# A hybrid decoder layer on one core: the convolution's last tap and bias from GpSimd to ScalarE

## The chip, the cores and the metric

The kernel runs on 1 core of one Trainium2 chip. A core has five engines that work side by side and wait for each other through semaphores: TensorE (PE in the profile; its weight loads are PEld), VectorE (DVE), ScalarE (ACT), GpSimd (POOL) and SyncE (SP), which here only issues DMAs. TensorE multiplies out of SBUF into banks of PSUM; VectorE and ScalarE read PSUM and SBUF. In this kernel GpSimd reads and writes SBUF alone. The metric is device time in microseconds from launch to end, as the median of several runs. A profile is of one execution more; it has a span, from its first to its last instruction, and a time of its own.

## The reference, cut to what matters

One layer (DEPTH is 1) of a trunk with two groups of heads, on a prompt of 2048 tokens and on 8 samples of one token, with D_MODEL 1024:

```python
ada = silu(c) @ w_ada + b_ada
shift, scale, gate = split(ada, 3)
hn = rmsnorm(x, g_norm) * (1 + scale) + shift
xa, za, q, k, v, glr, zg = split(hn @ w_in, SPLITS)

xp = concatenate([conv0, xa], axis=1)                    # 3 rows of the past, then xa
xc = conv_b + sum(xp[:, j:j + T] * conv_w[j] for j in range(4))
gx = sigmoid(xc @ w_gate_x + b_gate_x)                   # by blocks of 128 columns
ga = sigmoid(xc @ w_gate_a + b_gate_a)
log_a = 8 * ga * log_sigmoid(lru_lambda)
u = sqrt(-expm1(2 * log_a)) * (gx * xc)
h = scan(h = exp(log_a) * h + u)
y_lru = h * silu(za)

y_gla = rmsnorm(gated_linear_attention(q, k, v, glr)) * silu(zg)
x = x + gate * (concatenate([y_lru, y_gla]) @ w_out)
y = rmsnorm(x, g_final)
```

All data is float32. The change touches the line of `xc` (conv_w has four taps, the last of which multiplies the token's own `xa`), and, elsewhere, the sum `+ b_ada` for `gate`.

## The kernel before, in words

Activations lie with their features on the 128 partitions and tokens along the free axis. A float32 product is made of three fp32r products: each operand is split into a rounded high part (ScalarE) and the rest (VectorE), and hi*hi, hi*lo, lo*hi are added in PSUM. `project` (L636 to L649) does that for one tile of 128 columns of w_in and one segment of tokens: 24 matmuls into one of four PSUM banks called `acc`, at L642 to L644.

The prompt is worked in two halves of 1024 tokens. The first half has two segments of 512; the second has three, of 384, 384 and 264 (256 tokens of the prompt and the 8 samples). In each half the four GLA heads take turns with groups of RG-LRU tiles (`LRU_TILES`). The last two tiles of the second half come on their own, at L1606 to L1616, while the first operands of the output projection are already being prepared. From about 1122 us on the output projection (L1476) runs alone.

For one RG-LRU tile, `xa_unit` (L1232) projects a segment, lets ScalarE copy the bank to `xa` (L1244; three columns of the past stand ahead of it), and calls `conv` (L1130). There GpSimd writes `cv` = first tap times `xa` + bias (L1136), and VectorE adds the other three taps in place (L1138). With the past's three columns ahead, tap k reads `xa` from column c0 + k on; the last tap, k = 3, reads just the columns that the copy wrote. ScalarE then rounds `cv` to `xh` (L1161, or L1154 where it comes later) and VectorE makes the rest, `xl` (L1162, L1155). The eight samples of the second half have their own small steps (L1147, L1149). `gates` (L1164) comes two or three units later: six matmuls per segment into two banks (L1174 to L1176), ScalarE's Tanh out of them (L1177), then Exp, Tanh and Sqrt (L1181 to L1184, each change of function table costs a load), and on VectorE the products L1188 to L1190 and the scan L1192. L1188 is the last reader of `cv`. `xa`, `xh`, `xl` and `cv` have one buffer each, so a tile's `cv` is written when the tile before has been through L1188.

In the middle of the two halves `modulate` (L180) prepares the second half's input: PE transposes (L188), ScalarE applies scale and shift by partition out of PSUM (L190, L191, the function Identity), GpSimd rounds (L192), VectorE takes the rest (L193). At the start L209 is the same kind of step.

`out_weights` (L718) multiplies the gate into w_out and builds the sums that the last stage needs, in the gaps of all this. It works in two column halves. `begin(q)` loads the gate (`g`, L725), its bias (`bt`, L726) and the first weights, and four units later `add` (L729) adds the bias (L730). `bt` shares the one buffer of tag "t" with the sums of the step before.

What sets the order: the source calls things in an order of units. `after(u, f)` queues f until u units have passed, `tick` advances the count and calls what is due. Beneath that, the framework plans the order of each engine's queue from its own estimates of when each instruction would be ready; the order of the source is a priority. Inside an engine's queue the chip keeps the planned order: an instruction that waits holds up those behind it. Two things pin the plan: `in_order` ties every instruction of a block to the one before on its engine, and `behind(q)` (L662) ties what is issued under it behind the newest instruction that the source has put on engine q. SyncE's queue of DMAs is planned the same way. PSUM banks are given out by the plan, too: an `acc` tile takes whichever of the four banks comes free.

Of the kernel before, what the change touches and what calls it, by code (L numbers as in the profile page):

```python
# [11 lines left out]
AF = mybir.ActivationFunctionType  # L12
OP = mybir.AluOpType
# [31 lines left out]
def dram(ap, off, pattern):  # L45
    return bass.AP(tensor=ap.tensor, offset=ap.offset + off, ap=pattern)
# [3 lines left out]
def hybrid_kernel(ctx, tc, i, o):  # L50
    nc = tc.nc
    V, S, G, PE, SP = nc.vector, nc.scalar, nc.gpsimd, nc.tensor, nc.sync
# [365 lines left out]
    with tc.tile_pool(name="ada", bufs=1, side="right") as ap:  # L418
# [79 lines left out]
        with in_order():  # L498
# [24 lines left out]
            for c in range(1, 4):  # L523
                k = (2 * c, 2 * c + 1)
# [111 lines left out]
    def project(w, c0, n, mid=None):  # L636

        hi, lo, _ = w
        ps = acc()
        for kt in range(KT):  # L640
            a, b = hh[:, kt, c0:c0 + n], hl[:, kt, c0:c0 + n]
            PE.matmul(ps[:, :n], hi[:, kt], a, start=kt == 0, stop=False)  # L642
            PE.matmul(ps[:, :n], hi[:, kt], b, start=False, stop=False)  # L643
            PE.matmul(ps[:, :n], lo[:, kt], a, start=False, stop=kt == KT - 1)  # L644
            if mid and kt == 3:
                mid()
            if kt % 2:
                drip()
        return ps[:, :n]  # L649
# [12 lines left out]
    def behind(q):  # L662

        return tc.issue_after(next(x for x in reversed(list(nc.cur_bb.bb.instructions)) if x.engine == q.engine))
# [5 lines left out]
    def after(units, fn, gla=False):  # L670
        clock[1] += 1
        heapq.heappush(pend, (clock[0] + units, clock[1], fn, gla))

    def tick(units=1.0):
        clock[0] += units
        while pend and pend[0][0] <= clock[0]:
            heapq.heappop(pend)[2]()
# [40 lines left out]
    def out_weights():  # L718


        def begin(q):

            g = hp.tile([P, 2, 256], F32, tag="g", name="g")
            bt = hp.tile([P, 2, 256], F32, tag="t", name="bt")
            SP.dma_start(g, dram(gated, (8 + 32 * q) * 256, [[0, P], [64 * 256, 2], [1, 256]]))  # L725
            SP.dma_start(bt, dram(i["b_ada"], 2 * D + q * 256, [[0, P], [512, 2], [1, 256]]))  # L726
            r = load(8 * q)

            def add():  # L729
                V.tensor_tensor(g, g, bt, op=OP.add)  # L730
                after(0.5, lambda: step(8 * q, r, g))

            after(4, add)

        def where(s):

            return s // 8, s // 4 % 2, s % 4

        def load(s):
            q, f, m = where(s)  # L740
            r = hp.tile([P, 2, 2, 256], F32, tag="r", name="r")
            for a in range(2):
                k = CTS[f] + 4 * a + m
                SP.dma_start(r[:, a], i["w_out"][0, k * P:(k + 1) * P].rearrange("p (b n) -> p b n", b=2)[:, :, q * 256:q * 256 + 256])
            return r

        def one(ops, end):


            if phase[0] == 1:  # L750
                after(0.5, lambda: one(ops, end))
                return
            with behind(V):
                for f in ops[0]:
                    f()
            after(0.5, (lambda: one(ops[1:], end)) if ops[1:] else end)

        def step(s, r, g):
            t = hp.tile([P, 3, 256], F32, tag="t", name="t")
            b11, b12, b21, b22 = r[:, 0, 0], r[:, 0, 1], r[:, 1, 0], r[:, 1, 1]  # L760
            q, f, m = where(s)
            c = slice(q * 256, q * 256 + 256)

            def op(*a):
                return lambda: V.tensor_tensor(*a[:3], op=a[3])

            def split(n, x):
                p = hp.tile([P, 2, 256], F32R, tag="p", name="p", bufs=2)
                S.copy(p[:, 0], x)
                V.tensor_tensor(p[:, 1], x, p[:, 0].bitcast(F32), op=OP.subtract)  # L770

                def store2():
                    for h in range(2):
                        SP.dma_start(wd2[n, :, h, m, c], p[:, h].bitcast(F32))

                after(1.5, store2)

            def store():

                for x, ops in ((r[:, 0], (B11, T1)), (r[:, 1], (B21, B22)), (t, (T2, T3, T4))):  # L780
                    for n, k in enumerate(ops):
                        if not (f and k in (B22, T4)):
                            SP.dma_start(wd[f, k, :, m, c], x[:, n])
                if s % 8 < 7:
                    after(1, lambda: again(s + 1, g))
                elif q == 0:
                    after(1, lambda: begin(1))

            one([[op(r[:, 0], r[:, 0], g, OP.mult)], [op(r[:, 1], r[:, 1], g, OP.mult)],
                 [op(t[:, 1], b22, b12, OP.subtract), op(b12, b12, b11, OP.subtract)],  # L790
                 [op(t[:, 0], b22, b12, OP.subtract), op(t[:, 2], b21, t[:, 0], OP.subtract)]]
                + ([[lambda: split(0, b22)], [lambda: split(1, t[:, 2])]] if f else []), lambda: after(1, store))

        def again(s, g):
            r = load(s)
            after(1.5, lambda: step(s, r, g))

        begin(0)
# [322 lines left out]
    def lru_units(half, last_a=None):  # L1121
# [5 lines left out]
        def t_(tag, dt=F32, extra=0):  # L1127
            return lp.tile([P, TH + NS + extra], dt, tag=tag, name=tag)

        def conv(j, s, xa, cv, xh, xl):  # L1130
            c0, sn = SEGS[half][s]
            c = slice(c0, c0 + sn)
            cq = slice(c0, min(c0 + sn, TH))
            cw = [vecT[:, j, R_CW + k:R_CW + k + 1] for k in range(4)]
            cb = vecT[:, j, R_CB:R_CB + 1]
            G.tensor_scalar(cv[:, cq], xa[:, cq], cw[0], cb, op0=OP.mult, op1=OP.add)  # L1136
            for k in range(1, 4):
                V.scalar_tensor_tensor(cv[:, cq], xa[:, cq.start + k:cq.stop + k], cw[k], cv[:, cq],  # L1138
                                       op0=OP.mult, op1=OP.add)
            if c.stop >= TH:  # L1140
                if half == 0:
                    V.tensor_copy(xac[:, j], xa[:, TH:TH + 3])
                else:
                    V.tensor_copy(stT[:, j, 0:3], xa[:, TH:TH + 3])
                    V.tensor_copy(stT[:, j, 4:12], xa[:, TH + 3:TH + 3 + NS])
                    cs = vecT[:, j, R_CONV:R_CONV + 24].rearrange("p (b k) -> p b k", k=3)
                    V.tensor_scalar(cv[:, sm], xa[:, TH + 3:TH + 3 + NS], cw[3], cb, op0=OP.mult, op1=OP.add)  # L1147
                    for k in range(3):
                        V.scalar_tensor_tensor(cv[:, sm], cs[:, :, k], cw[k], cv[:, sm],  # L1149
                                               op0=OP.mult, op1=OP.add)  # L1150

            def split():
                with behind(S):
                    S.copy(xh[:, c], cv[:, c])  # L1154
                V.tensor_tensor(xl[:, c], cv[:, c], xh[:, c].bitcast(F32), op=OP.subtract)  # L1155

            if last_a or half == 0 and j == LRU_TILES[3][-1]:

                after(2, split)
            else:  # L1160
                S.copy(xh[:, c], cv[:, c])  # L1161
                V.tensor_tensor(xl[:, c], cv[:, c], xh[:, c].bitcast(F32), op=OP.subtract)  # L1162
# [69 lines left out]
        def xa_unit(t, s):  # L1232
            j = t.j
            if s == 0:
                t.xh = t_("xh", F32R, 48)
                t.one = lp.tile([P, 1], F32, tag="one", name="one")
                t.xl, t.xa, t.cv = t_("xl", F32R), t_("xa", extra=8), t_("cv")
                if half == 0:
                    V.memset(t.xa[:, :3], 0.0)
                else:  # L1240
                    V.tensor_copy(t.xa[:, :3], xac[:, j])
            c0, sn = SEGS[half][s]
            ps = project(t.wx, c0, sn)
            S.copy(t.xa[:, 3 + c0:3 + c0 + sn], ps)  # L1244
            conv(j, s, t.xa, t.cv, t.xh, t.xl)
            tick()
            if last_a is None:
                after(3 if j == LRU_TILES[3][-1] or half == 1 else 2, lambda: gates(t, [s]))
            elif s == len(SEGS[half]) - 1:
                after(3 if j == LRU_TILES[3][-1] else 2, lambda: gates(t, range(s + 1)))  # L1250
# [4 lines left out]
        def za_unit(t, s):  # L1255
# [3 lines left out]
            tick()  # L1259

        return xa_load, xa_unit, za_load, za_unit

    def lru(half, js):
# [539 lines left out]
    for n in range(2, 16):  # L1803
        g = n - 1
# [17 lines left out]
    for q in range(8):  # L1822
        g, k = 2 + q // 2, q % 2
# [63 lines left out]
```

## Time and profile before

| | us |
|---|---|
| median of 3 runs | 1462.96 |
| the three runs | 1461.14, 1462.96, 1467.99 |
| profiled execution: its time | 1460.23 |
| profiled execution: its span | 1458.5 |
| busy in the span: PE / DVE / ACT / POOL | 1431.1 / 1002.3 / 632.3 / 95.9 |
| mean granted TensorE clock | 0.997 |

The profile's page gives busy time of each engine, the chain of waits that ended last, and groups of instructions by line of the source. A group's row reads: line, engine, operation, output and inputs by the program's names with shape, count; then busy time, the mean of one in ns; then the idle time of the engine just before those instructions and what ended it. A row of the waits reads: who waited for whom, us in total, how often, the longest. A row of the timeline reads: start, duration, engine, line, operation, and in square brackets the engine's idle time before it and its releaser. Matmuls overlap in their pipeline, so the durations of single matmuls add up to more than their share of the time; idle time of PE is what counts.

### The profile page before, as it was taken

The numbers are of one execution on the slowest core, as the hardware profiler recorded it, in microseconds if no ns is written. First come the engines' busy times: TensorE is split into PE (matmuls) and PEld (weight loads), VectorE is DVE, ScalarE is ACT, GpSimd is POOL, SyncE is SP. The second block draws the span as 40 slices with busy tenths as digits, with TensorE's granted clock in tenths as the row PEclk, the third lists the DMA queues.
The fourth block names the chain that finished last, engine by engine and source line by source line (L and its number), as shares of the span: only waits on it lengthen the run. The fifth ranks groups of instructions, "written<-read, shape, count | busy, mean of one in ns | idle before, by whom it ended". The sixth has DMA issues, their size and how long they took to land.

```text
span 1458.5 us, 23166 instructions
## 1 busy us (share of the span) xinstructions
PE 1431.1 (98%) x8753; PEld 1269.5 (87%) x8753; DVE 1002.3 (69%) x2390; ACT 632.3 (43%) x1137; POOL 95.9 (7%) x116
## 2 busy tenths in 40 slices
PE   7999999999999999999999999999999999999997
PEld 6888888888898888999999999999998887788886
DVE  5756555765766778667567656576678986688886
ACT  4642532652454376533532552345156522154332
POOL 1200000100100013001001101010011000000000
PEclk9999999999999999999999999999999999999999
DMA  9755544645555664245644535463552767694452
GB/s 332 261 177 173 191 163 145 211 138 183 169 193 185 204 207 152 95 137 164 213 139 168 179 134 177 163 200 128 188 200 82 281 227 274 227 349 143 139 172 102
DMA packets 173606, 268.53 MB, mean 184 GB/s; under 512 B 10483, under 2 KB 126867, under 8 KB 171054
## 3 DMA queue, kind: packets, MB, share of 16 engines
q1 hardware_dynamic: 141093, 250.00, 50.3%
q10 hardware_dynamic: 32048, 16.00, 3.7%
q8 instruction: 69, 1.13, 0.3%
q0 software_dynamic: 352, 1.05, 0.2%
q14 instruction: 44, 0.35, 0.1%
HBM read 168.55 MB, written 98.52 MB: 183 GB/s over the span
## 4 chain that ended last, share of the span: by engine, by line
PE 48%; DVE 4%; ACT 2%; DMA 1%; POOL 0%; issue 0%; SPq 0%; ACTq 0%; DVEq 0%
PE acc L1476 12%; PE tp L1476 9%; PE acc L642 6%; PE acc L644 6%; PE acc L643 6%; PE acc L327 2%; PE acc L328 2%; PE acc L329 1%; DVE cv L1138 1%; PE po L975 1%; PE pss L1682 1%; PE tp L1040 0%; DMA w<-parts 0%; POOL cv L1136 0%; PE tp L941 0%
## 5 line engine op out<-in xcount | busy, mean ns | idle before, releaser
L642 PE MATMUL acc<-hh,w 128*128 128x384 f32 (+2 forms) x1256 | 446.7, 356 | 2.2 <-DMA w<-parts 1.3
L643 PE MATMUL acc<-hl,w 128*128 128x384 f32 (+2 forms) x1256 | 435.4, 347 | 0.0
L644 PE MATMUL acc<-hh,w 128*128 128x384 f32 (+2 forms) x1256 | 434.6, 346 | 0.0
L642 PEld LDWEIGHTS acc<-hh,w 128*128 128x128 f32 x1256 | 236.2, 188 | 24.2 <-DVE xb L881 3.0
L644 PEld LDWEIGHTS acc<-hh,w 128*128 128x128 f32 x1256 | 236.2, 188 | 19.4
L643 PEld LDWEIGHTS acc<-hl,w 128*128 128x128 f32 x1256 | 236.3, 188 | 19.2 <-issue 0.4
L1476 PE MATMUL acc<-w,a 128*128 128x512 f32 (+1 forms) x792 | 184.8, 387 | 0.0
L1476 PEld LDWEIGHTS acc<-w,a 128*128 128x128 f32 x792 | 146.9, 188 | 33.1 <-issue 3.4
L327 PE MATMUL acc<-w,hh 128*128 128x256 f32 (+1 forms) x508 | 145.8, 287 | 0.1
L329 PE MATMUL acc<-w,hl 128*128 128x256 f32 (+1 forms) x508 | 143.6, 283 | 0.2 <-DVE hl L216 0.2
L328 PE MATMUL acc<-w,hh 128*128 128x256 f32 (+1 forms) x508 | 143.4, 282 | 0.0
L1476 PE MATMUL tp<-w,a 128*128 128x512 f32 x564 | 136.1, 391 | 0.0
L1476 PEld LDWEIGHTS tp<-w,a 128*128 128x128 f32 x564 | 105.4, 188 | 26.7 <-issue 5.1
L1030 ACT ACTIVATE zs<-acc 128x512 f32<-128x512 f32 (+2 forms) x80 | 41.1, 513 | 173.9 <-PE acc L644 173.6
L1031 DVE SCALAR_TENSOR_TENSOR zs<-zs,acc 128x512 f32<-128x512 f32 (+2 forms) x80 | 46.3, 579 | 79.6 <-ACT zs L1030 79.4
L327 PEld LDWEIGHTS acc<-w,hh 128*128 128x128 f32 x508 | 96.3, 189 | 1.7 <-DVE vl L859 0.4
L329 PEld LDWEIGHTS acc<-w,hl 128*128 128x128 f32 x508 | 96.2, 189 | 0.4 <-DVE hl L216 0.4
L1138 DVE SCALAR_TENSOR_TENSOR cv<-xa,vecT,cv 128x512 f32<-128x512 f32 (+2 forms) x120 | 77.1, 650 | 27.4 <-POOL cv L1136 27.1
L328 PEld LDWEIGHTS acc<-w,hh 128*128 128x128 f32 x508 | 95.6, 188 | 0.2
L1136 POOL TENSOR_SCALAR cv<-xa,vecT 128x512 f32<-128x512 f32 (+2 forms) x40 | 49.0, 1224 | 607.2 <-ACT xa L1244 483.8
L1326 ACT CAST a<-s 128x512 fp32r<-128x512 f32 x61 | 36.5, 620 | 95.6 <-issue 36.2
L858 ACT CAST vh<-acc 128x256 fp32r<-128x256 f32 x56 | 20.7, 370 | 90.1 <-PE acc L329 71.1
(341 smaller groups left out, 2246.0 us busy)
## 6 DMA issues: line engine op xcount, KB each, us to landing
w<-parts SPq DMA_DIRECT2D x38, 1024.0 KB
parts<-w SPq DMA_DIRECT2D x37, 1024.0 KB
wr<-in_w_in_dram SPq DMA_DIRECT2D x44, 512.0 KB
a<-mixd SPq DMA_DIRECT2D x63, 256.0 KB
w<-wd SPq DMA_DIRECT2D x12, 1024.0 KB
wada<-in_w_ada_dram SPq DMA_DIRECT2D x16, 512.0 KB
r<-in_w_out_dram SPq DMA_DIRECT2D x32, 256.0 KB
mixd<-zs ACTq DMA_DIRECT2D x32, 256.0 KB
```

The source lines that it names most:

```text
L327: PE.matmul(ps, hh[:, kt, c], hi[:, kt % 4], start=kt == 0, stop=False)
L328: PE.matmul(ps, hh[:, kt, c], lo[:, kt % 4], start=False, stop=False)
L329: PE.matmul(ps, hl[:, kt, c], hi[:, kt % 4], start=False, stop=kt == KT - 1)
L642: PE.matmul(ps[:, :n], hi[:, kt], a, start=kt == 0, stop=False)
L643: PE.matmul(ps[:, :n], hi[:, kt], b, start=False, stop=False)
L644: PE.matmul(ps[:, :n], lo[:, kt], a, start=False, stop=kt == KT - 1)
L1030: S.activation(z, ps, AF.Tanh, scale=0.5)
L1031: V.scalar_tensor_tensor(z, z, 1.0, ps, op0=OP.add, op1=OP.mult)
L1136: G.tensor_scalar(cv[:, cq], xa[:, cq], cw[0], cb, op0=OP.mult, op1=OP.add)
L1138: V.scalar_tensor_tensor(cv[:, cq], xa[:, cq.start + k:cq.stop + k], cw[k], cv[:, cq], op0=OP.mult, op1=OP.add)
L1326: S.copy(t[:, 0, k], (low(t) if src is None else src)[:, k])
L1476: PE.matmul(ps, t[:, u, k], w[:, v, k, c], start=(q < 3 or ps is own) and (k, u, v) == (0, 0, 0), stop=(k, u) == (3, 1), skip_group_check= ...
```

## The change

GpSimd's step leaves `conv`. Instead ScalarE, which has just copied the projection's PSUM bank to `xa`, reads the same bank a second time and writes `cv` = last tap times the bank + bias, with the tap and the bias as scalars by partition. VectorE's three steps now add the taps 0, 1 and 2 out of `xa`. `conv` gets the bank `ps` as an argument for that. For the samples nothing changes. In `out_weights` the add of the bias is put under `behind(V)`: it is tied behind the VectorE instruction that the source issued before it.

```diff
@@ out_weights, begin
             def add():
-                V.tensor_tensor(g, g, bt, op=OP.add)
+                with behind(V):
+                    V.tensor_tensor(g, g, bt, op=OP.add)
                 after(0.5, lambda: step(8 * q, r, g))
@@ lru_units
-        def conv(j, s, xa, cv, xh, xl):
+        def conv(j, s, ps, xa, cv, xh, xl):
...
-            G.tensor_scalar(cv[:, cq], xa[:, cq], cw[0], cb, op0=OP.mult, op1=OP.add)
-            for k in range(1, 4):
+            S.activation(cv[:, cq], ps[:, :cq.stop - cq.start], AF.Identity, scale=cw[3], bias=cb)
+            for k in range(3):
                 V.scalar_tensor_tensor(cv[:, cq], xa[:, cq.start + k:cq.stop + k], cw[k], cv[:, cq],
                                        op0=OP.mult, op1=OP.add)
@@ xa_unit
             S.copy(t.xa[:, 3 + c0:3 + c0 + sn], ps)
-            conv(j, s, t.xa, t.cv, t.xh, t.xl)
+            conv(j, s, ps, t.xa, t.cv, t.xh, t.xl)
```

## The prediction

> **What bounds the kernel now.** I read the page's engine table first, then busy time by stage, then what TensorE (PE) waited for.
>
> ```profile
> span 1458.5 us, 23166 instructions
> PE 1431.1 (98%) x8753; PEld 1269.5 (87%) x8753; DVE 1002.3 (69%) x2390; ACT 632.3 (43%) x1137; POOL 95.9 (7%) x116
> ```
>
> PE is busy for 1431.1 us of 1458.5, so 27.4 us is idle. No edit of this change touches a matmul. The time can therefore fall only by what is taken out of these 27.4 us, and rise only by new idle time. The view of busy time by stage (columns: stretch, length, then PE, PEld, DVE, ACT, POOL busy, clock, DMA share, GB/s) says where they lie.
>
> ```profile
> 0.00:60.00 60.00, 52.31 (x506) 42.02 (x506) 37.88 (x128) 29.86 (x52) 9.54 (x17) 0.97 0.95 328
> 60.00:520.00 460.00, 459.63 (x2570) 396.61 (x2571) 291.62 (x657) 205.67 (x340) 17.97 (x16) 1.00 0.55 177
> 520.00:600.00 80.00, 77.13 (x509) 67.03 (x508) 62.39 (x134) 51.42 (x87) 18.29 (x20) 1.00 0.46 153
> 600.00:1076.00 476.00, 470.44 (x3406) 457.96 (x3405) 309.27 (x964) 188.71 (x377) 38.02 (x50) 1.00 0.50 166
> 1076.00:1122.00 46.00, 43.70 (x274) 41.96 (x273) 39.62 (x80) 31.17 (x55) 9.34 (x9) 1.00 0.34 121
> 1440.00:1458.50 18.50, 9.86 (x55) 8.46 (x53) 10.79 (x25) 4.11 (x11) 0.00 (x0) 0.83 0.24 93
> ```
>
> 7.7 us are lost in the first 60 us and 8.6 us at the end, where no convolution runs. Between 60 and 520 us it is 0.4 us, though POOL runs 16 instructions there, most of them convolution steps. Left for this change are 2.9, 5.6 and 2.3 us in the three stages from 520 to 1122 us: 10.7 us in all. The granted clock in them is 1.00, so there is no gain to be had from it either. PE's own waits (engine, what, for whom: us in all, times, longest) name the causes:
>
> ```profile
> PE tp L188 <- ACT hnf L191: 2.4, 3, 1.3
> PE tp L1040 <- DVE on L988: 1.8, 3, 1.1
> PE acc L642 <- DMA w<-parts: 1.3, 2, 1.0
> PE acc L642 <- DVE xb L881: 0.9, 1, 0.9
> PE acc L1174 <- ACT xa L1244: 0.8, 1, 0.8
> PE acc L1174 <- DVE zs L1031: 0.7, 2, 0.6
> ```
>
> None names the convolution's own result. It can matter only through the order of work on VectorE (DVE) and ScalarE (ACT), or through a PSUM bank held longer.
>
> **The change part by part.** Removed are 40 GpSimd (POOL) steps at L1136, and 40 ACT steps come in their place. VectorE keeps 120 tap steps of the same three forms, with the other three taps. The durations, by groups, for the old step and for ACT's same function (scale and bias by partition, out of PSUM) at L209 and L191:
>
> ```profile
> L1136 POOL TENSOR_SCALAR cv<-xa,vecT 128x512 f32<-128x512 f32 x16 | 22.1, 1380 | 457.8 <-ACT xa L1244 346.8 <-DVE rs L146 93.4 <-PE acc L644 17.6
> L1136 POOL TENSOR_SCALAR cv<-xa,vecT 128x384 f32<-128x384 f32 x16 | 18.9, 1184 | 131.3 <-ACT xa L1244 118.8 <-DVE tx L1188 12.4
> L1136 POOL TENSOR_SCALAR cv<-xa,vecT 128x256 f32<-128x256 f32 x8 | 8.0, 994 | 18.2 <-ACT xa L1244 18.2
> L209 ACT ACTIVATE hnf<-tp,Sh,Gm 128x512 f32<-128x512 f32 x6 | 4.3, 774 | 11.7 <-DVE Gm L489 11.7
> L191 ACT ACTIVATE hnf<-tp,Sh,Gm 128x256 f32<-128x256 f32 x16 | 9.0, 560 | 0.0
> DVE cv L1138 <- POOL cv L1136: 27.1, 21, 4.8
> ```
>
> ACT's step is 0.774 us for 512 columns, 0.560 for 256, and halfway, 0.667, for 384. Together 16 x 0.774 + 16 x 0.667 + 8 x 0.560 = 27.5 us, which takes ACT from 632.3 to 660 us, still 45%: beside PE, cost nothing by itself. POOL gives up 49.0 us. DVE loses 27.1 us of waiting, but DVE has 456 us of idle time, so only those waits count that end at PE. I go through PE's stalls one at a time.
>
> *The stall at 557.80.* PE's transposes wait for ACT, and ACT stood behind the rounding of this convolution:
>
> ```profile
> 546.55 0.57 ACT L1244 COPY xa<-acc 128x512 f32<-128x512 f32 x1
> 547.22 1.86 POOL L1136 TENSOR_SCALAR cv<-xa,vecT 128x512 f32<-128x512 f32 x1 [17.59 <-PE acc L644]
> 549.11 0.75 DVE L1138 SCALAR_TENSOR_TENSOR cv<-xa,vecT,cv 128x512 f32<-128x512 f32 x1 [0.68 <-POOL cv L1136]
> 556.21 0.62 ACT L1154 CAST xh<-cv 128x512 fp32r<-128x512 f32 x1 [4.37 <-DVE zs L1208]
> 557.80 0.66 PE L188 MATMUL tp<-ident,xt 128*128 128x128 f32 x4 [1.34 <-ACT hnf L191]
> ```
>
> ACT's step after its copy ends near 547.12 + 0.774 = 547.9 instead of 549.08. DVE's wait of 0.68 us goes, and everything down to 557.80 moves by that: -0.7 (bounds -1.3, the whole stall, and 0 if another DVE wait takes its place).
>
> *The three stalls at L1040, 1.8 us together.* Here the per-head norm's chain on DVE is interleaved with the taps of a tile's last segment. The middle and longest of them, with the POOL step in front:
>
> ```profile
> 925.51 0.95 POOL L1136 TENSOR_SCALAR cv<-xa,vecT 128x256 f32<-128x256 f32 x1 [2.89 <-ACT xa L1244]
> 929.64 0.59 PE L1040 MATMUL tp<-ident,on 128*128 128x128 f32 x3 [1.08 <-DVE on L988]
> ```
>
> 0.95 becomes 0.560: -0.4 here. The other two hold 1.8 - 1.1 = 0.7 us; half their saving reaches PE at best, -0.2. Term: -0.6 (bounds -1.8 and 0).
>
> [...]
>
> *The last tile pair, 1076 to 1122 us.* This is what speaks against the change. The buffer cv is single; its next write waits for the last reader, tx at L1188. That happens once:
>
> ```profile
> 1098.41 0.86 ACT L1244 COPY xa<-acc 128x384 f32<-128x384 f32 x2 [1.50 <-DVE cv L1138]
> 1098.94 0.45 PE L1174 MATMUL acc<-xh,wg 128*128 128x384 f32 x1 [0.81 <-ACT xa L1244]
> 1100.20 0.57 ACT L1177 ACTIVATE tx<-acc,hbx 128x384 f32<-128x384 f32 x1
> 1102.60 1.24 DVE L1188 SCALAR_TENSOR_TENSOR tx<-tx,cv 128x1032 f32<-128x1032 f32 x1
> 1103.93 1.69 POOL L1136 TENSOR_SCALAR cv<-xa,vecT 128x384 f32<-128x384 f32 x2 [12.45 <-DVE tx L1188]
> 1104.25 1.26 ACT L1183 ACTIVATE tg<-tg,lc 128x1032 f32<-128x1032 f32 x1
> 1104.63 0.62 DVE L1138 SCALAR_TENSOR_TENSOR cv<-xa,vecT,cv 128x384 f32<-128x384 f32 x1 [0.80 <-POOL cv L1136]
> ```
>
> POOL could wait 12.45 us with nothing queued behind it. ACT can't: behind the new step stand the six gate activations, Exp, Tanh and the next copies. Either ACT takes them first, and the step follows the Tanh that ends at 1105.51, to 1106.2: DVE's first tap is then 1.5 us later than 1104.63. Of this the second segment gives back some 0.4, as ACT's two steps (1.3 us) replace POOL's pair (1.69). DVE is 39.6 of 46 us busy in this stage, so I let the rest, +1.1, reach PE. Or ACT runs it between the two, and nothing is lost: 0. The two banks of this tile's first segments, free after the copy at about 1099.2 now, stay held until then. Six gate groups must pass through the other two banks meanwhile: from -0.8 (the stall at 1098.94 ends another way) to +1.9 (the third group waits from 1098.94 to the first gate activation's end, 1100.77 by its row). I take 0 for the banks and +1.1 for the step: the two ends lie about equally far.
>
> *The bias of the gates.* The add is tied behind the VectorE instruction written before it. Now:
>
> ```profile
> 715.77 0.69 DVE L730 TENSOR_TENSOR g<-g,bt 128x512 f32<-128x512 f32 x1 [6.86 <-DMA bt<-in_b_ada_dram]
> 718.75 0.41 PE L642 MATMUL acc<-hh,w 128*128 128x384 f32 x1 [0.92 <-DVE xb L881]
> ```
>
> DVE stands 6.86 us for this load, with two evictions of value tiles and the decay's first step behind it; PE pays 0.92 us. The add already follows the eviction of the sixth of eight value tiles, where the source has it (eight half units after its loads). So the tie keeps the wait: 0 (bounds -0.9, if the load comes earlier, and 0).
>
> Sum: -0.7 - 0.6 + 1.1 + 0 = -0.2 us. The profiled execution took 1460.23 us, so 1460.0; the median of three runs, 1462.96, is 2.7 above it, and from there the same sum gives 1462.8. I say 1462. With all bounds its own range runs from -1.3 - 1.8 - 0.8 - 0.9 = -4.8 to +1.1 + 1.9 = +3.0: 1458 to 1466.
>
> **Rivals.** 0.5% (7.3 us) is about what a measurement of this kernel can tell from no change.
>
> *Faster.* The order of each engine's work is planned anew, since a POOL step became an ACT step, and the plan happens to close the stalls of the whole middle. The 10.7 us bound it: 1452.3; with two thirds or more of it, 1452 to 1456. For it: the stalls are ten separate ones of at most 1.3 us, each on an order. Against: seven of the ten us would have to go, and I find 1.3 that hang on POOL.
>
> *Slower: a weight load falls late.* SyncE issues weight loads, stores and reloads in one planned order, and a store there waits for DVE. If the new plan sets such a store ahead of a weight load, PE stands.
>
> ```profile
> w<-parts SPq DMA_DIRECT2D x38, 1024.0 KB
> SPq L783 <- DVE r L765: 117.7, 22, 13.6
> SPq L294 <- PE acc L644: 77.6, 13, 22.7
> 849.62 6.63 DMA w<-parts
> ```
>
> The wait for a store is up to 13.6 us, and a load then takes 6.63 us. The one in the chain at 849.62 already costs PE 1.0 us, so at that place there is no slack, and each us that such a load starts later is lost. It decides from 7.3 us of delay, a little over half of one such wait; the whole of it gives +13.6: 1470 to 1477. Against it: two of 38 loads are late now, for 1.3 us.
>
> *The banks.* The hold at 1099 us costs more than 1.9, because the projection's third bank is caught too, for one convolution step chain (1106.2 - 1099.2 = 7 us, less 2 us of gates that go on): +3 to +7, 1466 to 1470. [...]
>
> *It doesn't do what it says.* ACT's plan sets the step not behind the copy but behind Sqrt and its table load; DVE waits as long for ACT as for POOL now. Time 1463, give or take 1.
>
> **How the numbers follow.** Forecast 0.40, no effect 0.06, banks 0.10: same 0.56. Late load 0.28: a plan that leaves only 10.7 us of idle time in the middle is easier to upset than to better. Faster 0.16. The range from 1453 to 1475 leaves out a quarter to a third of each of the two outer cases, 0.13 in all; the likeliest case alone has 1458 to 1466.
>
> **What would show it.** POOL's busy time falls to about 47 us, ACT's rises to 660; DVE's wait of 27.1 us for POOL is gone and a shorter one for ACT stands there; the stall at L188 shrinks below 1 us; in the last pair an ACT step on cv waits for DVE's tx. PE's waits for weights above 3 us, or idle time in the middle below 4 or above 18 us, would make me wrong.

## The result and the profile after

The changed kernel takes 1459.54 us (median of 19 runs, 1457.20 to 1464.15), the kernel before in the same comparison 1462.43 us (19 runs, 1460.34 to 1467.99). The ratio is 0.9977, 95% interval 0.9968 to 0.9986: a gain of 0.2%, real but within the 0.5% that I counted as no change. The profiled execution of the changed kernel took 1462.15 us (span 1460.4), 2.6 above its median; that of before took 1460.23, 2.2 below its own. So the two traces differ by +1.9 us where the medians differ by -2.9, and they must be read place by place. Of all the runs in this document one, of the kernel before with the bias load on GpSimd's queue, took 1766.68 us at a granted clock of 0.751 and is left out of the ratios.

The page of the changed kernel:

```profile
span 1460.4 us, 23147 instructions
PE 1434.0 (98%) x8753; PEld 1272.6 (87%) x8753; DVE 997.4 (68%) x2390; ACT 656.4 (45%) x1177; POOL 46.2 (3%) x76
```

PE's idle time fell from 27.4 to 26.4 us, but the same 8753 matmuls took 2.9 us longer: 1.9 us in sum. Busy time by stage of the changed kernel (columns as in the prediction), first the three middle stages, then four cuts of them:

```profile
520.00:600.00 80.00, 78.92 (x524) 69.13 (x523) 63.12 (x140) 54.58 (x92) 10.34 (x16) 1.00 0.48 155
600.00:1076.00 476.00, 469.85 (x3376) 457.71 (x3375) 305.33 (x958) 197.26 (x394) 17.79 (x32) 0.99 0.50 164
1076.00:1122.00 46.00, 44.07 (x281) 42.52 (x280) 38.93 (x79) 33.80 (x58) 1.31 (x2) 1.00 0.35 123
...
700.00:720.00 20.00, 17.59 (x136) 17.30 (x135) 9.97 (x33) 8.65 (x15) 0.00 (x0) 0.98 0.89 293
720.00:740.00 20.00, 19.87 (x122) 19.41 (x121) 9.71 (x29) 11.39 (x21) 0.86 (x2) 0.94 0.03 6
840.00:880.00 40.00, 37.99 (x256) 37.24 (x255) 20.49 (x61) 19.35 (x33) 0.89 (x2) 0.96 0.36 122
880.00:1076.00 196.00, 195.82 (x1396) 190.51 (x1395) 130.05 (x419) 76.73 (x162) 7.71 (x15) 1.00 0.54 175
```

The same cuts of the kernel before:

```profile
700.00:720.00 20.00, 19.08 (x151) 18.79 (x151) 10.74 (x31) 7.84 (x13) 0.00 (x0) 1.00 0.89 291
720.00:740.00 20.00, 19.86 (x133) 19.41 (x132) 12.31 (x37) 12.93 (x24) 2.25 (x4) 1.00 0.10 35
840.00:880.00 40.00, 38.84 (x275) 38.03 (x274) 22.38 (x64) 20.91 (x37) 2.49 (x4) 1.00 0.38 127
880.00:1076.00 196.00, 194.09 (x1382) 188.59 (x1381) 127.67 (x410) 71.57 (x150) 16.72 (x21) 1.00 0.52 174
```

Idle time of PE is the stretch less its busy time. It fell by 1.8 us in 520 to 600 (2.9 to 1.1), by 1.7 in 880 to 1076 and by 0.4 in the last pair. It rose by 1.5 in 700 to 720 and by 0.9 in 840 to 880, and the granted clock was 0.94 in 720 to 740 and 0.96 in 840 to 880, where it had been 1.00. What PE and VectorE waited for in the changed kernel:

```profile
PE acc L642 <- DVE f L905: 2.4, 1, 2.4
PE acc L642 <- DMA w<-parts: 1.9, 1, 1.9
PE acc L1175 <- ACT tx L1178: 1.6, 2, 1.3
PE tp L188 <- ACT hnf L191: 0.8, 1, 0.8
...
DVE cv L1139 <- ACT cv L1137: 1.7, 3, 1.1
```

L188 went from 2.4 to 0.8, the 1.8 at L1040 (now L1041) is gone altogether, and VectorE's 27.1 us of waiting in the convolution is 1.7. At L642, where the two rows shown in the prediction make 2.2 us, it is 4.3 us now. The place of the first gain, in the timeline of the changed kernel:

```profile
546.00 0.56 ACT L1245 COPY xa<-acc 128x512 f32<-128x512 f32 x1
546.47 0.78 ACT L1137 ACTIVATE cv<-acc,vecT 128x512 f32<-128x512 f32 x1
547.61 0.74 DVE L1139 SCALAR_TENSOR_TENSOR cv<-xa,vecT,cv 128x512 f32<-128x512 f32 x1
...
554.70 0.62 ACT L1155 CAST xh<-cv 128x512 fp32r<-128x512 f32 x1 [2.75 <-DVE zs L1209]
...
556.41 0.60 PE L188 MATMUL tp<-ident,xt 128*128 128x128 f32 x4
```

ScalarE's step takes 0.78 us where GpSimd's took 1.86, VectorE's wait of 0.68 is gone, and PE reaches L188 at 556.41 with no wait. Now the place of the loss, the stall near 718 us:

```profile
711.30 0.39 SPq L726 DMA_DIRECT2D bt<-in_b_ada_dram  x1
711.78 1.20 SPq L294 DMA_DIRECT2D w<-parts  x2
...
718.55 0.41 PE L642 MATMUL acc<-hh,w 128*128 128x384 f32 x1 [2.40 <-DVE f L905]
718.80 0.33 PE L643 MATMUL acc<-hl,w 128*128 128x384 f32 x1
718.97 0.47 PE L644 MATMUL acc<-hh,w 128*128 128x384 f32 x1
719.24 0.53 PE L642 MATMUL acc<-hh,w 128*128 128x384 f32 x1
719.56 0.53 PE L643 MATMUL acc<-hl,w 128*128 128x384 f32 x1
...
722.62 0.34 PE L644 MATMUL acc<-hh,w 128*128 128x384 f32 x1
722.79 0.34 PE L642 MATMUL acc<-hh,w 128*128 128x384 f32 x1
```

PE arrives 1.7 us earlier than before, but the matmuls go on at 718.55 as against 718.75. The traces' records of landings show what comes then: the first of the two weight loads lands at 718.42, in the kernel before at 718.62, and each time PE goes on 0.13 us after it. It was issued 0.94 us earlier than before (711.78 against 712.72) but took longer, 6.64 us against 5.90, and the gain of 520 to 600 is lost to it. Then, for 3.4 us, matmuls start every 0.32 us instead of 0.17, which costs about 1.6 us more. The same happens at 858.53, behind the 1.9 us wait for weights, which was 1.0 us before. There PE is not earlier but 1.3 us later than before, and the load itself took longer: 7.47 us against the 6.63 of the chain before. Why is open.

```profile
850.93 7.47 DMA w<-parts
```

The releaser named at 718.55, `f` on VectorE, is only the instruction that came last by semaphores; the landing, and the experiments below, show that it is the weight load behind `bt`.

### The profile page after: what moved, and what is told of

It is laid out like the page before. It is cut to its first block, busy times and chain, and to the rows that moved or that the text cites. A ratio compares the mean times of both kernels' runs of the same rounds, so it can differ in the third digit from the quotient of the medians.

```text
span 1460.4 us, 23147 instructions
## 1 busy us (share of the span) xinstructions
PE 1434.0 (98%) x8753; PEld 1272.6 (87%) x8753; DVE 997.4 (68%) x2390; ACT 656.4 (45%) x1177; POOL 46.2 (3%) x76
## 4 chain that ended last, share of the span: by engine, by line
PE 49%; DVE 3%; ACT 2%; DMA 2%; issue 0%; POOL 0%; SPq 0%; ACTq 0%; POOLq 0%; DVEq 0%
PE acc L1477 12%; PE tp L1477 9%; PE acc L642 6%; PE acc L644 6%; PE acc L643 6%; PE acc L327 2%; PE acc L328 2%; PE acc L329 1%; PE po L976 1%; DVE cv L1139 1%; PE pss L1683 1%; DMA w<-parts 1%; PE tp L1041 0%; DMA a<-mixd 0%; DMA mixd<-zs 0%
## 5 line engine op out<-in xcount | busy, mean ns | idle before, releaser
L642 PE MATMUL acc<-hh,w 128*128 128x384 f32 (+2 forms) x1256 | 448.1, 357 | 4.7 <-DVE f L905 2.4
L642 PEld LDWEIGHTS acc<-hh,w 128*128 128x128 f32 x1256 | 237.2, 189 | 27.4 <-DVE f L905 2.7
L158 ACT ACTIVATE junk<-on 128x256 bf16<-128x256 f32 x64 | 26.7, 417 | 85.2 <-DVE on L981 78.1
```

The costliest lines, as they stand in the source:

```text
L158: S.activation(junk[:m, :n], x, AF.Square, accum_out=out)
```

## The experiments

The kernel before ran beside each group of four: 1463.35 us (26 runs) with the first, 1463.45 (26) with the second, 1461.79 (15) with the third. Compare the ratios across groups, not the times.

| | us, median | ratio to before, 95% interval |
|---|---|---|
| the change | 1459.54 | 0.9977, 0.9968 to 0.9986 |
| convolution alone | 1458.95 | 0.9969, 0.9959 to 0.9980 |
| hold alone | 1463.59 | 0.9999, 0.9990 to 1.0008 |
| the change, bias load on GpSimd's queue | 1457.32 | 0.9956, 0.9941 to 0.9971 |
| first step on VectorE | 1460.32 | 0.9979, 0.9970 to 0.9988 |
| ScalarE's step out of SBUF | 1457.70 | 0.9958, 0.9945 to 0.9970 |
| a second step of ScalarE | 1458.63 | 0.9969, 0.9957 to 0.9981 |
| GpSimd's step put back, unread | 1460.96 | 0.9981, 0.9971 to 0.9992 |
| before, bias load on GpSimd's queue | 1465.97 | 1.0015, 1.0006 to 1.0025 |
| convolution alone, bias load on GpSimd's queue | 1459.58 | 0.9989, 0.9979 to 0.9999 |
| bias load moved, other buffer in the last pair | 1455.62 | 0.9960, 0.9947 to 0.9974 |
| bias load moved, ScalarE's step out of SBUF | 1456.27 | 0.9959, 0.9947 to 0.9972 |
| both of these | 1456.36 | 0.9956, 0.9944 to 0.9969 |

**Which part of the change does it.** Each part alone:

```diff
 convolution alone (from the changed kernel)
-                with behind(V):
-                    V.tensor_tensor(g, g, bt, op=OP.add)
+                V.tensor_tensor(g, g, bt, op=OP.add)
```

> The convolution's part of the change alone; the add of the gates' bias is not tied. Theory A (the gain is the shorter way from ScalarE's copy to VectorE's first tap, which ends PE's stalls at the head outputs' transposes, 1.8 us, and most of those at the second half's input, 2.4 to 0.8 us): 1459.5, give or take 1, ratio to before 0.998. Theory B (the gain is the moved add, whose wait of 6.86 us on VectorE is gone): 1462.4, ratio 1.000. If the untied add comes earlier in the plan than before, it is slower than before under both.

```diff
 hold alone (from the kernel before)
-                V.tensor_tensor(g, g, bt, op=OP.add)
+                with behind(V):
+                    V.tensor_tensor(g, g, bt, op=OP.add)
```

> The kernel before with the add tied and nothing else. Theory A: the time of before, ratio 0.999 to 1.001, since PE's stall near 718 us (0.92 us in the profile of before) waits for a weight load and not for the add. Theory B: 1459.5, ratio 0.998, and that stall is gone.

The convolution alone has the whole gain, and the hold alone has none. Yet the hold did move the add. In the convolution alone VectorE still stands for the bias, and longer than before; with the hold the add comes some 25 us later and waits for nothing. The add in the timelines of the convolution alone, and of the hold alone:

```profile
716.80 0.69 DVE L730 TENSOR_TENSOR g<-g,bt 128x512 f32<-128x512 f32 x1 [9.02 <-DMA bt<-in_b_ada_dram]
```

```profile
721.96 0.41 PE L642 MATMUL acc<-hh,w 128*128 128x384 f32 x1 [1.56 <-DMA w<-parts]
...
742.25 0.83 DVE L731 TENSOR_TENSOR g<-g,bt 128x512 f32<-128x512 f32 x1
```

With VectorE's wait gone, PE's stall near 720 us is still there, and now it is named for what it is: a late weight load. By the records of landings the load lands at 721.82, 0.14 us before PE goes on; in the convolution alone it lands at 719.21, 0.13 before PE goes on behind a stall of 2.6 us that is put down to VectorE there.

**The bias load and the weight load behind it.** SyncE issues `bt` just ahead of the weights, and `bt` waits for the buffer that it shares with a store's source: 1.7 us on SyncE in the kernel before and 1.1 in the changed one, until `wd<-t` has landed. Moved to GpSimd's queue:

```diff
-            SP.dma_start(bt, dram(i["b_ada"], ...))
+            G.dma_start(bt, dram(i["b_ada"], ...))
```

> The changed kernel with the load of the gates' bias (bt) issued on GpSimd's queue instead of SyncE's. Theory C (the stall near 718 us is a late weight load: SyncE stands before it for the bias' buffer, about 1.5 us): the weight load is issued about 1.5 us earlier, the stall of 2.4 us falls below 1.2 us and the granted clock stays at 1.00 between 720 and 740 us (0.94 in the changed kernel's profile); median 1 to 3 us below the changed kernel, ratio to before 0.9955 to 0.997. Rival (the stall waits for VectorE's chain of the decay, as the profile's releaser says): the stall stays at 2.4 us and the time at 1459.5.

The stall is gone. The two stretches in busy time by stage, and then the weights' issue in the timeline, both of the changed kernel with that load moved:

```profile
700.00:720.00 20.00, 20.00 (x154) 20.00 (x153) 9.99 (x32) 8.28 (x14) 0.76 (x1) 1.00 0.89 296
720.00:740.00 20.00, 19.87 (x137) 19.35 (x137) 13.94 (x40) 12.71 (x24) 2.47 (x4) 1.00 0.16 54
```

```profile
710.86 1.89 SPq L294 DMA_DIRECT2D w<-parts  x2
```

The weights are issued 0.9 us earlier, without 256 KB ahead of them, and the first load lands 2.5 us earlier, at 715.95 instead of 718.42. The bias now lands behind it, at 717.89, where the tied add doesn't wait for it. That the time falls with it is likely but not certain: the intervals of the two ratios (0.9941 to 0.9971, 0.9968 to 0.9986) overlap by a little. The same edit in two kernels without the hold:

> The kernel before, with nothing changed but that the load of the gates' bias is issued from GpSimd's queue and no longer from SyncE's. Theory 1 (the stall of 0.92 us near 718 us is a weight load that stands behind the bias load on SyncE): that stall goes or shrinks below 0.3 us, the stalls at L1040 (1.8) and L188 (2.4) stay, and the time falls by 0.5 to 1.5 us. Rival (that stall is the price of VectorE's wait for the bias): it stays, and the time with it.

> The changed kernel without the hold, so that VectorE stands at the add until the bias is there, and with the bias load on GpSimd's queue. Theory 1 (VectorE's wait reaches TensorE as soon as the bias lands late enough, as the 12.0 us wait did in the kernel before with the load on GpSimd's queue): a wait of 9 us or more at the add, a stall of 2 to 4 us behind it, 1459.5 to 1461.5. Rival (the wait is slack wherever it stands): as the changed kernel with the load on GpSimd's queue, 1457.3 give or take 1.2.

In the kernel before it made things worse, against both theories. On either queue the load waits for the store that reads its buffer (the releaser named is `wd<-t`). That store is issued at 709.87, in the kernel before at 707.48; the bias is issued at 714.99 instead of 712.24, behind the weights (713.86) instead of ahead of them, and lands 7.6 us after its issue, where before the add began 3.5 us after it. So VectorE waits 12.0 us at the add, until 722.60, and PE, whose banks VectorE should have emptied, stands 4.1. The two instructions in that kernel, then in the convolution alone with the load moved:

```profile
722.60 0.69 DVE L730 TENSOR_TENSOR g<-g,bt 128x512 f32<-128x512 f32 x1 [11.98 <-DMA bt<-in_b_ada_dram]
...
723.68 0.45 PE L642 MATMUL acc<-hh,w 128*128 128x384 f32 x1 [4.14 <-DVE vl L859]
```

```profile
718.85 0.69 DVE L730 TENSOR_TENSOR g<-g,bt 128x512 f32<-128x512 f32 x1 [10.75 <-DMA bt<-in_b_ada_dram]
...
719.93 0.44 PE L642 MATMUL acc<-hh,w 128*128 128x384 f32 x1 [2.90 <-DVE vl L859]
```

In both PE goes on 1.08 us after the add. In the kernel before it was 2.98 us after (718.75 against 715.77), so there VectorE had long been done, and the weights came last (landing at 718.62). With the load moved, the ratio is 0.9956 with the hold and 0.9989 without it, and the intervals lie apart: the hold is worth 0.3% once the weights no longer hide VectorE's wait, and nothing as long as they do.

**Why the convolution alone gains: place, GpSimd's work beside it, ScalarE or the bank.** First, any engine but GpSimd:

```diff
-            S.activation(cv[:, cq], ps[:, :cq.stop - cq.start], AF.Identity, scale=cw[3], bias=cb)
-            for k in range(3):
+            V.tensor_scalar(cv[:, cq], xa[:, cq], cw[0], cb, op0=OP.mult, op1=OP.add)
+            for k in range(1, 4):
```

> The changed kernel with the first of the four convolution steps on VectorE out of xa (first tap and bias), neither GpSimd nor ScalarE. VectorE gets some 14 us more work (40 steps of about 0.35 us), ScalarE 24 us less. Theory A (only the way from the copy to the first tap counts): as fast as the changed kernel or faster, 1457 to 1460. Rival (it is ScalarE as such: work taken off an engine chain near the limit): 1461 to 1464, with longer stalls between 1076 and 1122 us, where VectorE is 39 of 46 us busy.

VectorE alone is as fast as the change (0.9979 against 0.9977), and the stalls at L1041 are gone there too; L188 keeps 1.7 us. Then ScalarE out of SBUF instead of the bank:

```diff
-            S.activation(cv[:, cq], ps[:, :cq.stop - cq.start], AF.Identity, scale=cw[3], bias=cb)
-            for k in range(3):
+            S.activation(cv[:, cq], xa[:, cq], AF.Identity, scale=cw[0], bias=cb)
+            for k in range(1, 4):
```

> The changed kernel, but ScalarE's step reads the copy in SBUF with tap 0, and VectorE does taps 1 to 3: the projection's bank is free after the copy, and ScalarE's step waits for its own copy. Theory 1 (the gain comes from GpSimd's place in the chain being taken by a shorter step; out of which memory it reads is nothing): the same time as the changed kernel, 1459.5 give or take 1.5, no stall at L1041, about 1 us at L188. Rival (reading the bank is what shortens the way): 1461 or more, with a stall at L1041 or L188 back.

It is no slower either (0.9958), so reading the bank is not what gains. More load on ScalarE and on the banks, and GpSimd's load without its place in the chain:

```diff
 a second step of ScalarE
+            S.activation(xl[:, cq], ps[:, :cq.stop - cq.start], AF.Identity, scale=cw[3], bias=cb)
 GpSimd's step put back, unread
+            G.tensor_scalar(xl[:, cq], xa[:, cq], cw[0], cb, op0=OP.mult, op1=OP.add)
```

> The changed kernel with a second step of ScalarE for every segment, the same function out of the same bank into a buffer that is written over later: 27.5 us more on ScalarE, and the bank held for one step more. Theory 1 (ScalarE and the banks have room): within 1 us of the changed kernel. Rival (the banks, or ScalarE's own time): 3 to 7 us more, with new waits of PE for ScalarE in the three stages from 520 to 1122 us.

> The changed kernel with GpSimd's old 40 steps put back beside it, their results written to a buffer that is written over later, so that the convolution waits for none of them: GpSimd's busy time is as before, its place in the chain is not. Theory 1 (the place in the chain cost the time): as the changed kernel, 1459.5 give or take 1.5. Rival (GpSimd slowed VectorE by contention, and that is what went): VectorE's 512 taps back at about 768 ns, and 1461.5 or more.

The second step took ScalarE to 679.8 us and cost nothing that can be measured: ScalarE and the banks have room. With GpSimd's 40 steps put back, but read by nobody, the time stays at 1460.96 (0.9981, the upper end of what theory 1 gave), L1041 stays without a stall and L188 has 1.1 us. GpSimd is not quite out of VectorE's way there: VectorE writes the same buffer next and waited 1.8 us for it, in three places, against 27.1 in the kernel before. So it is the place in the chain, and not the load beside it, that makes these stalls. Groups of that kernel, VectorE's taps and GpSimd's step, then VectorE's taps in the changed kernel:

```profile
L1140 DVE SCALAR_TENSOR_TENSOR cv<-xa,vecT,cv 128x512 f32<-128x512 f32 x48 | 36.7, 765 | 0.1
...
L1138 POOL TENSOR_SCALAR xl<-xa,vecT 128x512 fp32r<-128x512 f32 x16 | 24.4, 1531 | 461.1 <-ACT xa L1246 271.2 <-DVE tg L1194 98.4 <-DVE rs L146 91.5
```

```profile
L1139 DVE SCALAR_TENSOR_TENSOR cv<-xa,vecT,cv 128x512 f32<-128x512 f32 x48 | 36.1, 751 | 0.1
```

With GpSimd's step put back, VectorE's tap of 512 columns took 765 ns instead of 751: 14 ns, or 0.7 us over 48 taps.

**The last tile pair.** `cv` of the last tile in another buffer, so that nothing waits for `tx` and the banks go back at once; first with ScalarE's step out of the bank, then with the step out of SBUF, without that buffer and with it (the bias load on GpSimd's queue in all three):

```diff
-                t.xl, t.xa, t.cv = t_("xl", F32R), t_("xa", extra=8), t_("cv")
+                t.xl, t.xa, t.cv = t_("xl", F32R), t_("xa", extra=8), (last_a() if last_a and j == LRU_TILES[3][2] else t_("cv"))
```

> The changed kernel with the bias load on GpSimd's queue, and with another buffer for cv in the last tile, so that in the last pair ScalarE's steps need not wait for tx and give the banks of the first two segments back at once. Theory 1 (the held banks make the stall of 1.6 us at the gates of the last pair, and the low clock behind it): that stall falls below 0.8 us, the clock there is 1.00, and the time is 1 to 2.5 us below 1457.3. Rival (ScalarE is late there for another reason, or what is won is lost later): 1457.3 give or take 0.8.

> ScalarE's step out of SBUF with tap 0, VectorE's taps 1 to 3, the hold, and the bias load on GpSimd's queue. Theory 1 (the late weight load near 718 us costs each version the same, and the order of the taps costs nothing): 1 to 2.5 us below the same kernel with the load on SyncE's queue (1457.7), so 1455.2 to 1456.7, no stall over 1 us near 718 us. Rival (the gain of that queue belongs to one plan and not to another, as the kernel before showed): 1457.5 or more.

> The kernel just named, and with it another buffer for cv in the last tile. Its banks are free after the copies anyway. Theory 1 (only the held banks matter in the last pair, not the wait for tx): within 0.8 us of the kernel just named. Rival (the wait for tx costs VectorE's chain itself): 1 to 2 us less.

The other buffer won nothing in either form (0.9960 against 0.9956; 0.9956 against 0.9959). In the first of these ScalarE, no longer kept waiting, takes its two steps ahead of the gate activations, and PE waits for those instead:

```profile
1093.92 0.68 ACT L1137 ACTIVATE xt<-acc,vecT 128x384 f32<-128x384 f32 x1
...
1094.65 0.54 PE L1175 MATMUL acc<-xh,wg 128*128 128x384 f32 x1 [1.95 <-ACT xt L1137]
1094.85 0.69 ACT L1137 ACTIVATE xt<-acc,vecT 128x384 f32<-128x384 f32 x1
1095.42 0.60 ACT L1178 ACTIVATE tx<-acc,hbx 128x384 f32<-128x384 f32 x1
```

So my theory of the held banks fell: the stall there was 1.58 with the banks held and is 1.95 with them free. Out of SBUF with the bias load moved, PE's wait near 718 us is gone too (20.00 of 20 us busy from 700 to 720), and the median is 1456.27. But its ratio, 0.9959, is that of the same kernel with the load on SyncE (0.9958): here the moved load gained nothing that can be measured. Five versions lie at 0.9956 to 0.9960, about 0.4% below the kernel before, and cannot be told apart.

## Why the prediction was right or wrong

The forecast was 1462 us, no change beyond 0.5%; it came out at 1459.54, inside the likeliest case's own range of 1458 to 1466. The bound held: only 10.7 us of idle time in the middle could move, and 1.6 of it did (9.2 left). The sum, -0.2, was too small a gain by 2.7 us against the medians; its terms were off in both directions.

- *What the sum left out.* That so small a sum came near is partly luck: +1.1 stood where idle time fell, and the loss that came stood in a rival. One premise failed, that the time can rise only by new idle time: in the trace 2.9 us came as longer busy time, with the granted clock at 0.50 in two spells of 3.41 us.
- *The stall at 557.80, -0.7.* Mechanism right, mis-sized: the three waits at L188 went from 2.4 to 0.8, -1.6. I priced only the one stall that I had traced. It went whole (1.34), a second of 0.28 too, and the third of 0.8 stayed. For the first I took VectorE's wait of 0.68; its first tap came 2.56 us after the beginning of ScalarE's copy and comes 1.61 us after it now, 0.95 less. On top of that the copy began 0.55 us earlier (546.00 against 546.55), while PE came to the transposes at the same time as before (556.41 against 556.46).
- *The three stalls at L1040, -0.6.* Mis-sized: all 1.8 us went. I took the difference of one short step, 0.95 to 0.560 us. With the convolution alone VectorE's taps and norm steps are interleaved anew, and the matmuls' order differs from before at three places. With ScalarE's step out of SBUF the matmuls keep the old order at 790.93 and 1066.62, and the stalls there (0.18 and 0.57) are gone all the same; at 929.64 (1.08) every version that leaves GpSimd out of the chain has another order, so what freed that one is open. Shown is that L1041 is free whenever nothing waits for a step on GpSimd, be the step on ScalarE or on VectorE.
- *GpSimd's step beside VectorE.* The step took very different times on the same 384 columns. In the kernel before it took 0.66 us at 1052.90, while VectorE ran L1045 and L980, and 3.23 at 810.92, while VectorE ran a tap and the scan:

```profile
1052.90 0.66 POOL L1136 TENSOR_SCALAR cv<-xa,vecT 128x384 f32<-128x384 f32 x1 [7.52 <-ACT xa L1244]
...
810.92 3.23 POOL L1136 TENSOR_SCALAR cv<-xa,vecT 128x384 f32<-128x384 f32 x1 [1.66 <-ACT xa L1244]
810.98 0.61 DVE L1138 SCALAR_TENSOR_TENSOR cv<-xa,vecT,cv 128x384 f32<-128x384 f32 x1
811.51 2.35 DVE L1192 TENSOR_TENSOR_SCAN tg<-xl,hc,tx 128x1024 f32<-128x1024 f32 x1
```

  At 814.15 GpSimd's step ends 0.3 us after VectorE's scan (813.86). VectorE's side lost 14 ns a tap with the step put back. That VectorE's work is what made the step long was not shown: no run changes only that. Whether a shorter step on GpSimd would have gained as much was not tried.
- *The last tile pair, +1.1.* The wrong branch: ScalarE ran the steps between Exp and Tanh (1105.78 to 1106.99), "nothing is lost", and idle time there fell by 0.4. VectorE's first tap came 2.32 us after the beginning of the product that frees `cv`, before 2.03. The banks' term, taken as 0, lies within its bounds (whose upper end, by its own rows, is 1.8 and not 1.9): the waits for ScalarE at these gates, 0.8 and 0.6, became 1.6 in two.
- *The bias of the gates, 0.* The price was right, the reading wrong twice. The tie does not keep the wait; it moves the add from 715.77 to 740.43. And the 0.92 us at 718.75 was not the add's price but a late weight load, which landed at 718.62 and which the releaser's name hid.
- *Rival, a weight load falls late.* It came about in part, by another way than a store. At 718 PE came 1.7 us earlier and the load landed only 0.2 earlier; at 858 PE came 1.3 later and the load, slower by 0.84, landed 2.1 later. The waits for weights are 4.3 us (1.9 by the profile's names, 2.4 by the landing), above the 3 that I had set as the mark for being wrong. In the profiled execution they cost 2.4 us of new idle time (1.5 and 0.9) and, with the lower clock, 2.9 of longer matmuls, and ate the gains of 1.8, 1.7 and 0.4. That the median is still 2.9 us below before I can't divide among places: there is one trace of each kernel, and whether the low clock and the slower loads come in each execution isn't known.
- *It doesn't do what it says, and the banks.* Excluded: POOL 46.2 and ACT 656.4 us (47 and 660 foretold), 27.1 us of waits down to 1.7, and a longer hold of every bank without a measurable cost.

## What to carry to other kernels

Where PE is 98% busy, price an edit at all its places, and then look at the next thing that arrives at a time of its own: here 1.7 us gained ahead of a weight load were lost at that load, which landed only 0.2 us earlier. A short step on an engine with free time can be the slowest link of a chain; look at its longest instruction, not at its mean (3.23 us against 1.18 for GpSimd's 384 columns, on an engine busy for 7%). When a wait is hidden behind another that ends later, removing it shows nothing: the hold alone gave 0.9999, and with the moved load 0.9956 against 0.9989 without it. And check a releaser's name against the landing of the loads that the instruction needs.

## What the runs showed of the hardware

The traces record the granted clock. In the changed kernel, ahead of its last 5 us, it is 0.50 three times, for 3.41 us each, from 12.46, 719.02 and 858.96 us on. These starts lie 207 and 41 such lengths apart (3.413 us by the record). In the 3.41 us before each of them PE had stood for 1.22, 2.41 and 1.88 us in all. After the second and the third, matmuls of 384 columns started every 0.32 us instead of 0.17, from which I estimate about 1.6 us lost each time. In the kernel before, ahead of its last 7 us, the clock is 0.50 once, for 3.41 us from 11.85 on, after 1.24 us of standing. In the convolution alone with the load moved PE stood longer at one stall, 2.90 us up to 719.93, and the clock stayed at 1.00 before and after it. Two stretches of the changed kernel, then two of that one:

```profile
715.61:719.02 3.41, 1.00 (x7) 0.71 (x6) 2.55 (x10) 2.23 (x4) 0.00 (x0) 1.00 1.01 411
719.02:722.43 3.41, 3.41 (x12) 3.41 (x11) 0.83 (x3) 1.04 (x2) 0.00 (x0) 0.50 0.29 117
...
700.00:720.00 20.00, 17.09 (x138) 16.78 (x137) 7.33 (x22) 7.55 (x12) 0.76 (x1) 1.00 0.88 280
720.00:740.00 20.00, 19.87 (x126) 19.25 (x127) 13.68 (x41) 12.51 (x23) 0.85 (x2) 1.00 0.03 10
```

So in these traces it was not the length of a stall that told whether the clock fell behind it: 2.40 us was followed by about 1.6 us of slower matmuls, and 2.90 us by none. What does tell is not shown here.
